# A decoder step on one core: pair 0 of the feed-forward part without Strassen products, and the attention's weight low parts made on VectorE

## The chip, the cores and the metric

The kernel runs on one core of a Trainium2 chip. The time is device microseconds of one execution. Before the change three runs gave 1425.21, 1429.11 and 1429.80 us; the median is 1429.11.

The engines are TensorE (products; PE in the rows, PEld its weight loads), VectorE (DVE), ScalarE (ACT), GpSimd (POOL) and SyncE (SP, whose queue issues nearly all transfers here). Each takes its instructions in the order in which the program gives them.

## The reference, cut to what matters

One layer of a hybrid decoder on 1024 prompt positions and 8 single-position samples, in fp32, model width 1024:

```python
hp = hp + mixer_block(rmsnorm(hp), ...)                      # gMLP heads and SSD heads, one output projection
mk, mv = mem_kv(mem_prompt, norm_mem, w_k, w_v)
hp = hp + cross_attn(rmsnorm(hp), mk, mv, w_q, w_xo)         # 4 heads of 256 into 256 memory tokens
hp = hp + (silu(hn @ w_gate) * (hn @ w_up)) @ w_down         # hn = rmsnorm(hp), hidden width 2816
```

The samples go the same way with caches of keys and values of their own, 256 tokens for each. A last norm follows.

## The kernel before, in words

**Products in two parts.** An fp32 operand is split into a high part, cast to fp32r, and a low part, the difference. A product of two such operands is three products, high by high, high by low, low by high (`mm3`, L164). Weights come in panels of 128 x 1024, eight k-tiles of 128 x 128 side by side. `split_panel` (L139) makes both parts of a panel: ScalarE casts the high part (L146), and the low part (L147) is a subtraction on GpSimd or VectorE. The tags `whi` and `wlo` have three buffers, `raw` two, and `ahead` splits a panel one ahead of its use and loads one more.

**Columns.** Activations stand with features on partitions. The 1032 columns (1024 positions, 8 samples) are chunk 0 (512), chunk 1 (256) and chunk 2 (264).

**Order of the stages.** Memory keys and values, mixer projections with the SSD chunks between, output projection (`wo`), and then the attention in five passes over weight panels: `qc` (queries of chunk 2), `qa` (chunk 0), `qb` (chunk 1), `xoa` (output projection of chunk 0) and `xob` (chunks 1 and 2). While the products of `qa`, `qb` and `xoa` run, the attention of chunk 2, 0 and 1 is threaded between them by `later`, which counts products: scores (`m_sc`), row maximum on VectorE (`mx`), exponential on ScalarE (`ex`), transposes (`m_pt`), split of the probabilities (`pTh` on ScalarE, `pTl` on VectorE), product with the values (`m_pv`), split of its result (`oh`, `ol`). The samples' attention lies in the same passes: in `qa` VectorE multiplies key caches with spread queries (`kc<-kc,qb`, L1000), in `xoa` value caches with spread probabilities (L1102); each needs a transfer of 512 KB for `qb` and two for `kc`. The passes `qa`, `qb` and `xoa` have eight panels each, whose low parts GpSimd makes; those of `qc` and `xob` VectorE makes.

**From attention to FFN.** `norm_evac` (L906) adds each result of `xob` to the residual, sums the squares on VectorE, and after the eighth panel of a chunk asks `lagged_rstd` (L256) for the reciprocal root mean square: the column sums (`m_csn`) are placed `LAG_N[0]` = 14 products later, the transposes that spread the result over the partitions (`m_crn`) `LAG_N[1]` = 20 products behind the sums. Between them lie a square root on ScalarE and five short operations on VectorE, the last of which writes `crvn`. `quarters` then scales the residual into four quarters for each of two column halves q: q = 0 folds columns 0 to 255 and 256 to 511 (chunk 0), q = 1 chunks 1 and 2. A quarter `b11`, `b21`, `b12`, `b22` is a half of the features by a half of those columns. `combine` (L1187) makes the seven operands `P1` to `P7` of a Strassen scheme from them, by four differences and seven splits. The quarters of q = 1 take the buffers of those of q = 0.

**The pairs.** The 22 hidden tiles are 11 pairs. For a pair and a weight (gate `g`, up `u`), `gate_up` (L1255) runs seven products of half the features; `prepare` (L1226) forms the weight's four sums (`ws`, L1237 to L1240) and splits each of the seven weight operands (`fw`, 128 x 512). Sums are made on VectorE for the first four items and on GpSimd for later ones. The evacuations combine the seven results (L1283 to L1298). The items are, in order, `g0` and `u0` for q = 0 alone, then each further pair for both q, and `g0`, `u0` for q = 1 behind pair 6. `xob` ends at about 718 us, item `g0` starts there, and item `u0` at about 739.

**The order of instructions.** The program is written in stages, but a scheduler with a time model puts each engine's instructions in order before the launch; `tc.high_priority()` prefers a group and `later` gives the product behind which a group may be issued. Names with `m_` and `g_` are the two groups of PSUM banks.

The line for the engine of the low parts is L147:

```python
(nc.gpsimd if i == 0 or P_QA <= i < P_XO[1] else nc.vector).tensor_tensor(lo[:, s], r[:, s], f(hi[:, s]), op=ALU.subtract)
```

Of the kernel before, what the change touches and what calls it, by code (L numbers as in the profile page):

```python
# [9 lines left out]
F32R = mybir.dt.float32r  # L10
BF16 = mybir.dt.bfloat16
AF = mybir.ActivationFunctionType
ALU = mybir.AluOpType
# [30 lines left out]
def hymba_step(ctx: ExitStack, tc: tile.TileContext, I, O):  # L44
# [24 lines left out]
    def f(ap):  # L69
        return ap.bitcast(F32)  # L70
# [43 lines left out]
    P_QA = add(I["w_q"], 8)  # L114
    P_QB = add(I["w_q"], 8)
    P_XO = [add(I["w_xo"], 8) for _ in range(2)]
    NPAIR = NF // 2

    raws, split = {}, {}
# [19 lines left out]
    def split_panel(i):  # L139
        if i in split or i >= len(panels):  # L140
            return
        load_panel(i)
        r = raws[i]
        hi, lo = (wp.tile([P, D], F32R, tag=x, name=f"w{x[1]}{i}") for x in ("whi", "wlo"))
        for s in (slice(0, 512), slice(512, D)) if i == 0 else (slice(0, D),):
            nc.scalar.copy(hi[:, s], r[:, s])  # L146
            (nc.gpsimd if i == 0 or P_QA <= i < P_XO[1] else nc.vector).tensor_tensor(lo[:, s], r[:, s], f(hi[:, s]), op=ALU.subtract)  # L147
        n = D // panels[i].shape[1]
        split[i] = (hi.rearrange("p (k n) -> p k n", n=n), lo.rearrange("p (k n) -> p k n", n=n))

# [752 lines left out]

    def norm_evac(accs, H, gi, XN, spill, nm, use=None, tmps=None):  # L906

        acc = {}
        pool = nrm

        def evac(j, ci, ps):
            w = CH[ci][1] - CH[ci][0]
            h = H[ci][j // 4][:, j % 4, :]
            with tc.high_priority():
                nc.vector.tensor_add(h, h, ps)
                if j == 0:
                    acc[ci] = accs[ci].tile([P, 512 if accs[ci] is nrm else w], F32, tag=f"acc{'' if accs[ci] is nrm else ci}", bufs=1, name=f"{nm}acc{ci}")
                    nc.scalar.activation(acc[ci][:, :w], h, AF.Square)
                else:
                    sq = pool.tile([P, 512], F32, tag="nsq", bufs=2, name=f"{nm}sq{ci}_{j}")  # L920
                    nc.scalar.activation(sq[:, :w], h, AF.Square)
                    eng = nc.gpsimd if j < 6 and nm == "n1" else nc.vector
                    eng.tensor_tensor(acc[ci][:, :w], acc[ci][:, :w], sq[:, :w], op=ALU.add)
            if spill is not None and j % 4 == 3:
                nc.sync.dma_start(spill[:, j - 3 : j + 1, CH[ci][0] : CH[ci][1]], H[ci][j // 4])
            if j == 7:
                lagged_rstd(LAG_N, lambda rb: (use or normed)(ci, rb[0]), pool, [[acc[ci]]], ci, 1.0 / D, f"{nm}{ci}")

        def normed(ci, rb):
            w = CH[ci][1] - CH[ci][0]  # L930
            hi = [hs(ci, F32R, f"{nm}h{ci}_{i}") for i in range(2)]
            lo = [hs(ci, F32R, f"{nm}l{ci}_{i}") for i in range(2)]
            for k in range(KT):
                i, kk = k // 4, k % 4
                tmp = n2.tile([P, 512], F32, tag=tmps[0], bufs=2, name=f"{nm}t{ci}_{k}")
                nc.vector.scalar_tensor_tensor(tmp[:, :w], H[ci][i][:, kk, :], vecT[:, k, gi : gi + 1], rb[:, :w], op0=ALU.mult, op1=ALU.mult)
                split_from(hi[i][:, kk, :], lo[i][:, kk, :], tmp[:, :w], nc.gpsimd if k % 2 else None)
            XN[ci] = xof((hi, lo))

        return evac  # L940

    quarters = None
    with ExitStack() as c2:
# [185 lines left out]

        H2 = [None] * 3  # L1130
        n3accs = [nrm] * 3
        ev_xo = norm_evac(n3accs, H2, V_FFN, None, h2_d, "n3", lambda ci, rb: quarters(ci, rb))
        XO = [lambda k, ci=ci: (OS[ci][0][k // 4][:, k % 4, :], OS[ci][1][k // 4][:, k % 4, :]) for ci in range(3)]

        def h2(ci):
# [12 lines left out]
    with ExitStack() as c3:  # L1148
# [8 lines left out]

        def operand(q, nm):

            if nm == ORDER[-1]:  # L1160
                return [n3.tile([P, 4, 264], F32R, tag="op", bufs=4, name=f"s{nm}{x}{q}")[:, :, : WQ[q]] for x in "hl"]
            if q == 0:
# [24 lines left out]
        def combine(q):  # L1187
# [4 lines left out]
                XQ[q][nm] = operand(q, nm)  # L1192
                split_from(*XQ[q][nm], src, eng)

            part("P1", b11)
            nc.vector.tensor_tensor(b11, b12, b11, op=ALU.subtract)
            part("P5", b11)
            nc.vector.tensor_tensor(b11, b22, b11, op=ALU.subtract)
            part("P6", b11)
            part("P2", b21)  # L1200
            nc.vector.tensor_tensor(b12, b22, b12, op=ALU.subtract)
            part("P7", b12)
            nc.vector.tensor_tensor(b21, b21, b11, op=ALU.subtract)
            part("P4", b21)
            part("P3", b22)


        items = [(x, 0, (0,)) for x in "gu"]
        for fp in range(1, NPAIR):
            items += [(x, fp, (0, 1)) for x in "gu"] + ([(x, 0, (1,)) for x in "gu"] if fp == 6 else [])  # L1210
        wraw, wsum, wop = {}, {}, {}
# [9 lines left out]

        def order_of(n):

            return ORDER if n > 3 else ("P1", "P2", "P6", "P7", "P5", "P4", "P3")

        def prepare(step):  # L1226

# [4 lines left out]
            (a11, a12), (a21, a22) = ((t[:, 0:512], t[:, 512:D]) for t in wraw[n])  # L1232
            nm = order_of(n)[o]
            if nm == "P6":
                eng = nc.vector if n < 4 else nc.gpsimd
                s1, s2, s3, s4 = wsum[n] = [n3.tile([P, 512], F32, tag="ws", bufs=4, name=f"ws{n}_{i}") for i in range(4)]
                eng.tensor_tensor(s1, a21, a22, op=ALU.add)  # L1237
                eng.tensor_tensor(s2, s1, a11, op=ALU.subtract)  # L1238
# [76 lines left out]
                    differences.append(lambda q=q, r=res[q]: down_operands(fp, q, r))  # L1315

        differences = []

        def down_operands(fp, q, r):

# [100 lines left out]
            return t[:, 0, i], t[:, 1, i]  # L1421

        stage(plan_of(P_XO[1], 8, first=(1, 2), last=(1, 2), chunks=(1, 2)), XO, ev_xo, name="xob")
        for n in range(len(items)):
            gate_up(n, between_of(n))
        form_differences()
# [212 lines left out]
```

## Time and profile before

| what | value |
|---|---|
| median of three runs | 1429.11 us (1425.21 to 1429.80) |
| profiled execution | 1433.45 us, span 1431.7 us |
| mean granted TensorE clock | 0.984 |
| TensorE busy | 1373.5 us, 96% of the span, 10291 products |
| VectorE busy | 967.6 us, 68% |
| ScalarE busy | 627.3 us, 44% |
| GpSimd busy | 365.5 us, 26% |

The profile is of one execution. The span is from the first to the last instruction; the execution's own time is 1.75 us longer. Busy shares are means over stages with different limits, so the rows below are read stage by stage. The granted clock is a share of 2.4 GHz: 1.00 is 2.4 GHz and 0.50 is 1.2 GHz; a value between is a mean over a stretch. In a row of a group, the number behind the comma is the mean length of one instruction in ns, and behind the second bar stands the idle time of the engine in front of the group. Names are `output<-inputs` with their buffer numbers left out.

### The profile page before, as it was taken

Reading aid. Unit: us, or ns where it says so; the run is one execution under the profiler, and the core shown is the slowest. Engines: PE = TensorE matmul, PEld = TensorE weight load, DVE = VectorE, ACT = ScalarE, POOL = GpSimd, SP = SyncE. Lnnn points to the kernel's source line nnn. Section 1 sums busy time; section 2 is a strip of 40 time slices with the busy share of each in tenths; the row PEclk is TensorE's granted clock in tenths of the full one; section 3 lists DMA queues with packets and bytes.
Section 4 is the critical chain, followed back from the end, with each engine's and each line's share of the span. In section 5 each row is a group of like instructions: output and inputs, shape, how many; then the busy total and the mean of one; then the engine's idle time right before and its main releaser. Section 6 shows DMA issues by size and latency. Waiting matters only on the chain. (4 is left out here: it accounts for less than half of the span.)

```text
span 1431.7 us, 26080 instructions
## 1 busy us (share of the span) xinstructions
PE 1373.5 (96%) x10291; PEld 1308.1 (91%) x10291; DVE 967.6 (68%) x2021; ACT 627.3 (44%) x1141; POOL 365.5 (26%) x289
## 2 busy tenths in 40 slices
PE   8999999999999989999979999999899999999997
PEld 8889988899998968978979999999899999999997
DVE  7875689734524876578988766676765665655685
ACT  5666545234423545744464332232332343544654
POOL 3321122201121524320001434334443431003020
PEclk9999999999999999999999999999999999999998
DMA  8531243311733487377324554434546569655664
GB/s 301 186 96 61 91 126 104 97 45 48 248 133 99 154 288 269 106 269 276 104 89 144 170 159 138 142 118 140 170 159 201 171 189 317 206 184 171 203 194 133
DMA packets 145531, 232.67 MB, mean 163 GB/s; under 512 B 8328, under 2 KB 91880, under 8 KB 145024
## 3 DMA queue, kind: packets, MB, share of 16 engines
q1 hardware_dynamic: 145264, 230.94, 49.8%
q8 instruction: 81, 1.33, 0.4%
q14 instruction: 42, 0.34, 0.1%
q10 hardware_dynamic: 144, 0.05, 0.0%
HBM read 179.16 MB, written 51.81 MB: 161 GB/s over the span
## 5 line engine op out<-in xcount | busy, mean ns | idle before, releaser
L146 ACT CAST wh<-wr 128x1024 fp32r<-128x1024 f32 (+1 forms) x85 | 88.0, 1038 | 85.3 <-PE g_gv L170 25.1
L275 ACT CAST fw<-ws 128x512 fp32r<-128x512 f32 x96 | 59.2, 620 | 137.8 <-POOL ws L1238 61.6
L276 DVE TENSOR_TENSOR fw<-ws,fw 128x512 fp32r<-128x512 f32 x96 | 88.9, 928 | 41.3 <-ACT fw L275 41.0
L147 DVE TENSOR_TENSOR wl<-wr,wh 128x1024 fp32r<-128x1024 f32 x59 | 75.9, 1289 | 28.3 <-ACT wh L146 28.1
L147 POOL TENSOR_TENSOR wl<-wr,wh 128x1024 fp32r<-128x1024 f32 (+1 forms) x26 | 62.8, 2415 | 112.2 <-ACT wh L146 67.3
L275 ACT CAST fw<-fr 128x512 fp32r<-128x512 f32 x72 | 44.5, 618 | 79.5 <-PE m_uZ L170 20.7
L1237 POOL TENSOR_TENSOR ws<-fr 128x512 f32<-128x512 f32 x20 | 26.8, 1341 | 200.4 <-DMA fr<-in_w_gate_dram 120.8
L276 DVE TENSOR_TENSOR fw<-fr,fw 128x512 fp32r<-128x512 f32 x72 | 59.5, 826 | 9.6 <-ACT fw L275 9.1
L1542 PE MATMUL m_d<-xP,dwhi 128*128 128x264 f32 x448 | 64.1, 285 | 0.0
L276 DVE TENSOR_TENSOR dwlo<-dw,dwhi 128x1024 fp32r<-128x1024 f32 x32 | 39.8, 1245 | 35.1 <-ACT dwhi L275 35.0
L1542 PE MATMUL g_d<-xP,dwhi 128*128 128x256 f32 x448 | 63.0, 283 | 0.0
L276 DVE TENSOR_TENSOR xP<-xsP,xP 128x512 fp32r<-128x512 f32 (+2 forms) x84 | 55.0, 696 | 11.4 <-ACT xP L275 9.8
L170 PE MATMUL m_uY<-sP,fw 128*128 128x264 f32 (+1 forms) x432 | 58.4, 284 | 2.1 <-DVE fw L276 1.5
L170 PE MATMUL g_gY<-sP,fw 128*128 128x256 f32 (+1 forms) x432 | 58.4, 283 | 1.7 <-DVE t L1292 1.7
L1542 PEld LDWEIGHTS m_d<-xP,dwhi 128*128 128x128 f32 x448 | 58.5, 189 | 0.0
L1542 PEld LDWEIGHTS g_d<-xP,dwhi 128*128 128x128 f32 x448 | 57.7, 191 | 0.0
L170 PEld LDWEIGHTS m_uY<-sP,fw 128*128 128x128 f32 x432 | 54.6, 189 | 2.7 <-DVE fw L276 1.7
L170 PEld LDWEIGHTS g_gY<-sP,fw 128*128 128x128 f32 x432 | 54.3, 190 | 2.4 <-DVE t L1292 2.3
L1304 POOL TENSOR_TENSOR u<-u,g 128x512 f32<-128x512 f32 (+1 forms) x22 | 30.1, 1372 | 100.4 <-DVE u L1296 99.5
L275 ACT CAST dwhi<-dw 128x1024 fp32r<-128x1024 f32 x32 | 33.6, 1051 | 48.7 <-PE m_d L1542 38.5
L275 ACT CAST xP<-xsP 128x512 fp32r<-128x512 f32 (+2 forms) x84 | 45.2, 588 | 21.4 <-DMA xsP<-x_d 12.2
L170 PE MATMUL m_gY<-sP,fw 128*128 128x264 f32 x360 | 49.2, 285 | 4.9 <-DVE t L1292 4.9
(520 smaller groups left out, 3918.5 us busy)
## 6 DMA issues: line engine op xcount, KB each, us to landing
xsP<-x_d SPq DMA_DIRECT2D x35, 520.0 KB, 5.6
wr<-in_w_q_dram SPq DMA_DIRECT2D x24, 512.0 KB, 4.0
fr<-in_w_gate_dram SPq DMA_DIRECT2D x24, 512.0 KB, 3.6
fr<-in_w_up_dram SPq DMA_DIRECT2D x24, 512.0 KB, 3.7
dr<-in_w_down_dram SPq DMA_DIRECT2D x22, 512.0 KB, 6.4
s_d<-ds SPq DMA_DIRECT2D x22, 512.0 KB, 3.2
wr<-in_w_in_dram SPq DMA_DIRECT2D x20, 512.0 KB, 4.0
dw<-s_d SPq DMA_DIRECT2D x20, 512.0 KB, 4.5
```

The source lines that it names most:

```text
L146: nc.scalar.copy(hi[:, s], r[:, s])
L147: (nc.gpsimd if i == 0 or P_QA <= i < P_XO[1] else nc.vector).tensor_tensor(lo[:, s], r[:, s], f(hi[:, s]), op=ALU.subtract)
L170: ins = nc.tensor.matmul(ps, lhs(k)[a], rhs(k)[b], start=(fresh and i == 0), stop=(i == n - 1), skip_group_check=not (fresh and done))
L275: nc.scalar.copy(dst_hi, src)
L276: (eng or nc.vector).tensor_tensor(dst_lo, src, f(dst_hi), op=ALU.subtract)
L1237: eng.tensor_tensor(s1, a21, a22, op=ALU.add)
L1304: nc.gpsimd.tensor_tensor(t, t, gates[q][:, 1, :, :], op=ALU.mult)
L1542: nc.tensor.matmul(ps[:, : WQ[q]], wdn[n](k)[a], x_at(nm, q, k)[b], start=(i == 0), stop=(i == 3 * NPAIR - 1))
```

## The change

Two things change. Pair 0 on q = 0 leaves the Strassen scheme: its four panels (two of `w_gate`, two of `w_up`) are split as other panels are, and `first_pair`, which stands between `xob` and the remaining items, multiplies each with both column halves, whose operands are the split quarters `P1`, `P2` (half 0) and `B12`, `P3` (half 1). `combine(0)` makes these four splits first and the differences behind them; `B12` is new and lies in two of the four `gu` buffers. The sums for items `g1` and `u1` stay on VectorE. The spread of the third norm is placed 44 products behind its sums in place of 20. And the low parts of all panels but the first are made on VectorE.

```diff
+    P_G0 = add(I["w_gate"], 2)
+    P_U0 = add(I["w_up"], 2)
...
-            (nc.gpsimd if i == 0 or P_QA <= i < P_XO[1] else nc.vector).tensor_tensor(lo[:, s], r[:, s], f(hi[:, s]), op=ALU.subtract)
+            (nc.gpsimd if i == 0 else nc.vector).tensor_tensor(lo[:, s], r[:, s], f(hi[:, s]), op=ALU.subtract)
...
-                lagged_rstd(LAG_N, lambda rb: (use or normed)(ci, rb[0]), pool, [[acc[ci]]], ci, 1.0 / D, f"{nm}{ci}")
+                lagged_rstd(lag, lambda rb: (use or normed)(ci, rb[0]), pool, [[acc[ci]]], ci, 1.0 / D, f"{nm}{ci}")
...
-        ev_xo = norm_evac(n3accs, H2, V_FFN, None, h2_d, "n3", lambda ci, rb: quarters(ci, rb))
+        ev_xo = norm_evac(n3accs, H2, V_FFN, None, h2_d, "n3", lambda ci, rb: quarters(ci, rb), lag=(14, 44))
...
+            if nm == "B12":
+                return [n3.tile([P, 4, 264], F32R, tag="gu", bufs=4, name=f"s{nm}{x}{q}")[:, :, : WQ[q]] for x in "hl"]
...
-            part("P1", b11)
+            if q == 0:
+
+                for nm, b in (("P1", b11), ("P2", b21), ("B12", b12), ("P3", b22)):
+                    part(nm, b)
+            else:
+                part("P1", b11)
...
-        items = [(x, 0, (0,)) for x in "gu"]
+        items = []
...
-            return ORDER if n > 3 else ("P1", "P2", "P6", "P7", "P5", "P4", "P3")
+            return ORDER if n > 1 else ("P1", "P2", "P6", "P7", "P5", "P4", "P3")
...
-                eng = nc.vector if n < 4 else nc.gpsimd
+                eng = nc.vector if n < 2 else nc.gpsimd
...
+        def first_pair():
+
+            for x, p0 in (("g", P_G0), ("u", P_U0)):
+                r = piece(f"{x}0_0")[:, :, :256].rearrange("p (j h) n -> p j h n", j=2)
+                for j in range(2):
+                    ahead(p0 + j)
+                    if p0 + j == P_U0:
+                        load_pair(0)
+                    if p0 + j == P_U0 + 1:
+                        for s in range(3):
+                            prepare(s)
+                    hi, lo = split[p0 + j]
+                    for half in range(2):
+                        ps = (gbank, mbank)[half](f"{x}0_{j}_{half}")
+                        ops = [XQ[0][nm] for nm in (("P1", "P2"), ("B12", "P3"))[half]]
+                        mm3(ps[:, :256], lambda k: (hi[:, k, :], lo[:, k, :]), lambda k: tuple(t[:, k % 4, :] for t in ops[k // 4]), range(KT))
+                        with tc.high_priority():
+                            if x == "g":
+                                nc.scalar.activation(r[:, j, half, :], ps[:, :256], AF.Silu)
+                            else:
+                                nc.vector.tensor_mul(r[:, j, half, :], gates[0][:, j, half, :], ps[:, :256])
+                gates[0] = r if x == "g" else None
+            differences.append(lambda: down_operands(0, 0, r))
...
         stage(plan_of(P_XO[1], 8, first=(1, 2), last=(1, 2), chunks=(1, 2)), XO, ev_xo, name="xob")
+        first_pair()
```

## Rows read from the trace of the kernel before

**Rows 1.** Stretches: length; busy PE, PEld, DVE, ACT, POOL (instructions); clock; transfer share; GB/s.

```profile
500.00:560.00 60.00, 52.90 (x276) 44.21 (x275) 43.66 (x162) 27.66 (x59) 18.07 (x9) 0.97 0.89 306
...
560.00:606.00 46.00, 46.00 (x379) 45.36 (x378) 22.93 (x59) 34.96 (x91) 21.47 (x9) 1.00 0.35 107
...
606.00:660.00 54.00, 50.58 (x268) 42.66 (x267) 42.52 (x149) 23.92 (x60) 12.30 (x5) 0.94 0.86 301
...
660.00:718.00 58.00, 58.00 (x451) 56.28 (x450) 52.55 (x117) 25.87 (x41) 0.25 (x2) 1.00 0.43 135
...
725.00:740.00 15.00, 5.67 (x45) 5.42 (x44) 12.26 (x34) 9.38 (x13) 0.00 (x0) 0.83 0.22 70
...
515.00:520.00 5.00, 4.69 (x18) 3.95 (x19) 1.70 (x5) 2.55 (x6) 1.78 (x1) 0.66 0.90 340
...
630.00:635.00 5.00, 5.00 (x12) 3.94 (x13) 4.94 (x23) 2.80 (x8) 0.00 (x0) 0.50 0.85 261
```

**Rows 2.** Waits of TensorE, 720 to 790: total us, times, longest.

```profile
PE m_crn L279 <- DVE crvn L224: 8.0, 1, 8.0
PE g_gY L170 <- DVE t L1292: 1.3, 1, 1.3
PE g_gX L170 <- DVE fw L276: 1.1, 1, 1.1
```

**Rows 3.** Instructions in order of time, 717 to 745: start us, length us.

```profile
723.81 0.50 PE L236 MATMUL m_csn<-ones,n3acc 128*128 128x1 f32 x4
...
729.27 0.16 DVE L224 RECIPROCAL crvn<-rsan 128x2 f32<-128x2 f32 x1
...
730.32 0.73 PE L236 MATMUL m_csn<-ones,n3acc 128*128 128x1 f32 x6
...
738.76 0.18 DVE L224 RECIPROCAL crvn<-rsan 128x3 f32<-128x3 f32 x1
...
739.61 2.67 PE L170 MATMUL m_uX<-sP,fw 128*128 128x256 f32 x12
```

**Rows 4.** Chain of waits: start us, us, what (a group of twelve products).

```profile
1140.70 1.43 PE g_uX L170 x12
```

**Rows 5.** VectorE groups, 718 to 748 and (last) 660 to 718: busy us, mean ns.

```profile
L276 DVE TENSOR_TENSOR fw<-ws,fw 128x512 fp32r<-128x512 f32 x7 | 4.8, 689 | 0.0
...
L1237 DVE TENSOR_TENSOR ws<-fr 128x512 f32<-128x512 f32 x2 | 1.4, 681 | 0.1
...
L1285 DVE TENSOR_TENSOR t<-t,g_gY 128x256 f32<-128x256 f32 x1 | 0.4, 423 | 0.0
...
L147 DVE TENSOR_TENSOR wl<-wr,wh 128x1024 fp32r<-128x1024 f32 x8 | 9.8, 1223 | 0.0
```

**Rows 6.** Waits of TensorE, 500 to 560 and (last) 610 to 660.

```profile
PE m_pv L170 <- DVE pTl L276: 3.5, 3, 2.0
...
PE m_pt L279 <- DVE pTl L276: 0.9, 1, 0.9
...
PE g_xoa L170 <- ACT ex L1028: 2.9, 1, 2.9
```

**Rows 7.** Instructions in order of time, 524 to 536: GpSimd beside VectorE.

```profile
526.70 2.59 POOL L147 TENSOR_TENSOR wl<-wr,wh 128x1024 fp32r<-128x1024 f32 x1 [6.09 <-ACT wh L146]
...
526.96 2.62 DVE L1000 SCALAR_TENSOR_TENSOR kc<-kc,qb 128x256 f32<-128x256 f32 x1
```

**Rows 8.** VectorE groups: 500 to 560 (first), 606 to 660 (two), 660 to 718 (two).

```profile
L1000 DVE SCALAR_TENSOR_TENSOR kc<-kc,qb 128x256 f32<-128x256 f32 x64 | 31.9, 561 | 8.2 <-DMA qb<-q_d 8.2
...
L1102 DVE SCALAR_TENSOR_TENSOR kc<-kc,qb 128x256 f32<-128x256 f32 x50 | 23.4, 524 | 6.1 <-DMA qb<-p_d 6.1
...
L923 DVE TENSOR_TENSOR n3acc<-n3acc,n3sq 128x512 f32<-128x512 f32 x4 | 5.6, 1405 | 0.7 <-ACT n3sq L921 0.7
...
L1102 DVE SCALAR_TENSOR_TENSOR kc<-kc,qb 128x256 f32<-128x256 f32 x14 | 5.1, 424 | 0.0
...
L923 DVE TENSOR_TENSOR n3acc<-n3acc,n3sq 128x512 f32<-128x512 f32 x3 | 2.1, 698 | 0.0
```

More of the change, by code (lines that the diff above doesn't have):

```diff
@@ L901, in hymba_step, with norm_evac @@
         stage([([(P_GU + j, j)], (0, 1, 2)) for j in range(2)] + [([(P_GU + j, j) for j in (2, 3)], (0, 1, 2))], X, ev_um, name="gu")
-    def norm_evac(accs, H, gi, XN, spill, nm, use=None, tmps=None):
+    def norm_evac(accs, H, gi, XN, spill, nm, use=None, tmps=None, lag=LAG_N):
         acc = {}
@@ L1199, in combine @@
             part("P6", b11)
-            part("P2", b21)
+            if q == 1:
+                part("P2", b21)
             nc.vector.tensor_tensor(b12, b22, b12, op=ALU.subtract)
@@ L1204, in combine @@
             part("P4", b21)
-            part("P3", b22)
-        items = [(x, 0, (0,)) for x in "gu"]
+            if q == 1:
+                part("P3", b22)
+        items = []
         for fp in range(1, NPAIR):
```

## The prediction

> **What bounds the kernel now.** I first read the stretches of the attention and of the passage into the feed-forward part (FFN) [rows 1]: in the pass `qb` (560 to 606) and in the last projection pass `xob` (660 to 718) TensorE is busy all the time; in `qa` (500 to 560) it misses 7.1 us, in `xoa` (606 to 660) 3.4 us, and from 725 to 740 it works for 5.67 us of 15. So products bound this kernel, and what can be won are the holes. The reader is to see in these rows that VectorE is the engine beside the holes: 52.55 of 58 us in `xob`, 12.26 of 15 in the largest hole. The waits of TensorE after 720 come next [rows 2]: 8.0 us for `crvn`, the reciprocal root mean square of the last column chunk, and 1.3 and 1.1 us for sums and weights that VectorE was late with. The order of time inside that hole [rows 3] shows why: the column sums of the chunk are done at 731.05, `crvn` at 738.94, because ScalarE and VectorE had the first pair's Strassen work in front of it, while TensorE had the transposes of `crvn` next in its order and nothing it could take instead. The waits of the attention passes [rows 6] and the durations of VectorE's sample products there [rows 7, 8] are the second field.
>
> **Part 1: the first pair by plain products.** TensorE: before, gate and up of pair 0 on columns 0 to 255 and 256 to 511 folded together are 2 x 7 groups of 12 products, 168; after, 2 weights x 2 panels x 2 halves x 24, 192. A group of 12 takes 1.43 us [rows 4], so 24 more cost **+2.9 us**, all on the path.
>
> VectorE: it loses 14 low parts of 0.69 (9.7), eight sums of 0.68 (5.4) and 11 evacuations of 0.42 (4.6); it gains four panel low parts of 1.22 (4.9), one operand split more, `B12` (1.2), and four gate products of 0.42 (1.7) [rows 5]. That is 19.7 less against 7.8 more, 11.9 us of relief between about 700 and 750, where it is full. Besides, the combined operands of columns 0 to 511 (four differences and their four splits) are not due at 718 any more but when pair 1 begins, some 25 us later. That relief is cover, and no term of its own: it lets the waits of 1.3 and 1.1 us go and keeps the operands of columns 512 to 1031 from becoming late, though pair 1 starts earlier. ScalarE's work shrinks as well (four wide casts for 14 narrow ones, one operand more), GpSimd loses two products, and SP issues four weight loads of 512 KB as before, panels in place of pairs, so I cost these at nothing; the cover is that all three have idle time here, and without it a late weight would cost what rows 2 show for one, 1.1 us. `B12` sits in two of the four buffers of gate results, which the results of pair 1 take next; these are first written two groups after pair 0's last product, so nothing waits.
>
> The wait for `crvn`: 192 products that need nothing from that chunk now lie behind the sums, and the transposes are placed 44 products behind them in place of 20. That is 5.3 us at 0.119 each, where before it was 2.4. The two chains from sums to `crvn` in the trace took 5.1 (724.31 to 729.43) and 7.9 us (731.05 to 738.94) [rows 3]. At 5.3 us the first fits and the second would leave 2.6. So of 8.0 + 1.3 + 1.1 us of waits, and 1.1 us that the first group behind the hole lost at the low clock (2.67 us against 1.43 plus its tail [rows 3, 4]; granted 0.83 on average from 725 to 740 [rows 1], so part of it at 1.2 GHz), 11.5 in all, 2.6 stay. **Part 1: 2.9 - 11.5 + 2.6 = -6.0 us.** Ends: -8.6 with no wait left, +0.5 with the 8.0 and the 1.1 back.
>
> **Part 2: low parts on VectorE.** 24 panels (`w_q` twice, `w_xo` once) move, each 1.22 us there [rows 5], so VectorE gets 29.3 us. What it loses shows in rows 7: the GpSimd operation runs from 526.70 to 529.29, and the sample product that VectorE started inside it took 2.62 us, where a like product takes 0.42 with GpSimd idle [rows 8]. By the means [rows 8], 64 products in `qa` lost (561 - 424) ns each, 8.8 us; 50 in `xoa` 5.0; four square sums there (1405 - 698) ns, 2.8. So 16.6 us of stretching go, and the net is +12.7 us of VectorE time.
>
> Where it lies: in `qb` VectorE is busy for 22.93 of 46 us and TensorE waits for nothing [rows 1], so eight low parts there cost nothing; if that idle time were gone they would cost up to 9.8. In `qa` 8.8 us go and 9.8 come, but a stretch always falls on a product with a softmax step queued behind it, while the low part can stand in the 16 us in which VectorE is idle there (it is made long before use: three buffers deep, and no wait of TensorE names it). In `xoa` GpSimd makes five low parts [rows 1], so 6.1 us come and 7.8 go. No row shows the new order of VectorE's queue, so I bound the gain: at best all waits that have a stretched chain in front go, 3.5 + 0.9 in `qa` and 2.9 in `xoa` [rows 6], and with them the low clock behind (0.66 and 0.50 of 5 us [rows 1], 1.7 and 2.5 us): 11.5. At worst 0, and below that the third rival. I take about half, 3.0 for `qa` and 2.5 for `xoa` (1.7 us of net relief and some of the clock), nearest to the row of stretched products that the waits follow. **Part 2: -5.5 us.**
>
> The plain exchange of engine time speaks against this part: 29.3 us more on an engine that is nearly full in `xoa`, for 16.6. The Trainium skill's page "Perfetto Trace Analysis", section "Optimizing Scalar/DVE Operations", says that work may well go from a saturated VectorE to GpSimd, though the two share an SBUF read port, so that moving between them might not help. By its first half the part would cost up to the third rival's price, by its second nothing. This trace agrees with the second half: 2.62 against 0.42 us.
>
> **Sum.** -6.0 - 5.5 = -11.5 us. The profiled execution took 1433.45 us (span 1431.7), so 1421.9 for a like one; that execution is 4.3 above the median of 1429.11, and against the median the forecast is **1417.6 us**. A measurement of this kernel tells some 0.3%, 4.3 us, from no change.
>
> **Rivals.**
> *The low parts win nothing.* For it: the chains in `qa` also wait for the sample loads, with the transfer engines busy for 0.89 of that stretch [rows 1]; what VectorE gains it would then wait for data. Against: TensorE's waits stand behind stretched products, not behind the loads alone. Only part 1 counts: 1429.1 - 6.0 = 1423.1.
> *The norm's wait stays.* If ScalarE's table changes between SiLU and square root or the eight products of chunk 1 get into the chain again, it takes longer than 44 products cover, and the 8.0 + 1.1 return: part 1 is +0.5, with part 2 1424.1, without it 1429.6. For it: 7.9 us is longer than 5.3. Against: VectorE has 11.9 us less to do.
> *VectorE's queue becomes the bound (slower).* In `qa` and `xoa` each low part is 1.22 us in front of a row maximum or a low part of probabilities, and TensorE waits for it. It decides where the chain has no slack left, as the waits of 3.5, 0.9 and 2.9 show for some places; with all 13 exposed, 15.9 - 6.0 = +9.9, 1439.0. Against: GpSimd's operation held the same queue for longer. That first half of the page's sentence points here; I give it no more than the rows do.
>
> **Chances.** Forecast 0.50; nothing from part 2 0.22; norm's wait 0.14; queue 0.12; something unseen 0.02. The range runs from near the best ends (1429.1 - 8.6 - 11.5 = 1409) to the norm's wait without part 2 (1429.6): 1411 to 1430, which leaves out the queue and a little below. Faster by over 0.3% (under 1424.8): 0.50 + 0.18 of the second case + 0.05 of the third = 0.73. Within 0.3%: 0.04 + 0.09 + 0.02 = 0.15. Slower: 0.12.
>
> **What would show it.** Right: TensorE busy without a hole of over 3 us between 715 and 750, pair 0 as 192 products, the wait for `crvn` at 2.6 us or less; sample products at a mean near 424 ns in `qa` and `xoa`, the wait of 2.9 us in `xoa` under 2 and no stretch at half clock behind it. Wrong: a wait of 5 us or more for `crvn`, TensorE waiting for `pTl` or `ex` more than 7.3 us in `qa` and `xoa` together, or any wait for `wl`. The forecast fails outright if the FFN's later pairs, which I take as unchanged, get new waits for weights.

## The result, and the profile after

The changed kernel takes **1412.06 us** (median of 4 runs, 1410.90 to 1412.72), the kernel before, run beside it, 1429.45 us (4 runs, 1425.21 to 1432.05). The ratio is **0.9872**, 95% interval 0.9854 to 0.989: 18.3 us of 1429 are gone (15.7 to 20.9), where the prediction said 11.5. The profiled execution took 1412.27 us (span 1410.4). Two more measurements of the same program, in the experiments below, gave 0.9854 and 0.9861.

The page of the changed kernel, part 1: busy time of each engine, its share, instructions.

```profile
PE 1369.1 (97%) x10315; PEld 1305.8 (93%) x10315; DVE 957.9 (68%) x2021; ACT 626.1 (44%) x1131; POOL 304.1 (22%) x263
```

The kernel before had 10291 products on TensorE; 24 more are there, 192 in place of 168 for the first pair. GpSimd lost 61 us of work. VectorE, which spends 29 us on what it took over, is not busier (957.9 against 967.6 us): the plain pair takes 11.6 us off it (956.0 in e1 below), and the rest is made up by operations that are no longer stretched.

The stretches of the changed kernel: first and last us, length, busy time of the engines, granted clock, DMA share. They are cut where TensorE starts its first product of `qa`, `qb`, `xoa`, `xob`, of the first pair and of the second.

```profile
489.60:551.10 61.50, 58.43 (x308) 48.85 (x306) 49.37 (x181) 31.97 (x67) 3.63 (x3) 1.00 0.88 315
551.10:587.90 36.80, 36.80 (x314) 36.78 (x313) 24.36 (x46) 26.42 (x64) 0.00 (x0) 1.00 0.49 159
587.90:658.20 70.30, 68.92 (x400) 59.83 (x399) 57.58 (x208) 36.08 (x90) 0.00 (x0) 1.00 0.73 263
658.20:708.00 49.80, 49.38 (x410) 48.99 (x409) 43.70 (x82) 26.13 (x40) 0.25 (x2) 1.00 0.43 138
708.00:732.50 24.50, 24.50 (x209) 24.50 (x208) 18.21 (x42) 15.77 (x22) 0.00 (x0) 1.00 0.29 88
```

The same cuts in the kernel before:

```profile
489.40:557.00 67.60, 60.50 (x307) 50.24 (x306) 51.51 (x174) 32.08 (x67) 25.68 (x13) 0.97 0.85 295
557.00:596.90 39.90, 39.90 (x340) 39.87 (x339) 18.13 (x43) 29.57 (x72) 19.46 (x8) 1.00 0.42 136
596.90:670.80 73.90, 70.47 (x387) 60.20 (x386) 59.86 (x207) 34.91 (x87) 14.71 (x6) 0.95 0.71 250
670.80:718.10 47.30, 47.30 (x398) 47.30 (x397) 41.85 (x77) 21.91 (x34) 0.25 (x2) 1.00 0.44 131
```

Work slides from one pass into its neighbour (`qb` lost 3.1 us and `xob` gained 2.5 while TensorE was busy nearly all through), so only the sum of the four passes compares well: 228.7 us before, 218.4 after, **10.3 us less**. In the traces of the two further measurements of this program (e3, e11) the passes take 216.1 and 215.9 us, 12.6 and 12.8 less. The first pair takes 24.5 us without a gap; before, from its first product to the second pair's first it was 30.0, with two groups of twelve (2.9) still to come, so 32.9: **8.4 us less**. Both stretches of low clock, 0.97 in `qa` and 0.95 in `xoa`, are gone. The rest of the FFN differs by 3 us between the two profiled executions: TensorE's listed waits behind 740 us sum to 17.1 us before and 14.2 after, spread over many small ones.

Waits of TensorE in the changed kernel, 489 to 740: total, times, longest. These are all of them.

```profile
PE m_pt L281 <- ACT ex L1041: 2.4, 2, 1.6
PE m_pv L172 <- DVE pTl L278: 1.0, 1, 1.0
PE m_pv L172 <- ACT pTh L277: 0.5, 1, 0.5
PE g_xob L172 <- ACT oh L277: 0.4, 1, 0.4
PE m_pv L172 <- ACT ex L1030: 0.4, 1, 0.4
```

Of the 3.5 us for `pTl` [rows 6] 1.0 are left; the 2.9 for `ex` in front of `xoa` [rows 6] and the 8.0 for `crvn` [rows 2] have no successor. Why there is none for `crvn` shows in TensorE's and VectorE's order of time (start, length):

```profile
712.16 0.50 PE L238 MATMUL m_csn<-ones,n3acc 128*128 128x1 f32 x4
...
716.31 0.38 PE L281 MATMUL m_crn<-ident,crvn 128*128 128x128 f32 x2
716.53 0.73 PE L238 MATMUL m_csn<-ones,n3acc 128*128 128x1 f32 x6
...
722.90 0.18 DVE L226 RECIPROCAL crvn<-rsan 128x3 f32<-128x3 f32 x1
...
723.63 0.49 PE L281 MATMUL m_crn<-ident,crvn 128*128 128x128 f32 x3
```

From the last column sum (717.26) to `crvn` (723.08) it is still 5.8 us, against 7.9 [rows 3], but TensorE has the plain pair's products for all of it.

VectorE's groups after, `qa` (first two) and `xoa` (last two): busy us, mean ns, idle before.

```profile
L1002 DVE SCALAR_TENSOR_TENSOR kc<-kc,qb 128x256 f32<-128x256 f32 x64 | 23.2, 419 | 8.0 <-DMA qb<-q_d 7.8 <-DVE pTl L278 0.3
L149 DVE TENSOR_TENSOR wl<-wr,wh 128x1024 fp32r<-128x1024 f32 x9 | 11.0, 1217 | 2.0 <-ACT wh L148 2.0
...
L1104 DVE SCALAR_TENSOR_TENSOR kc<-kc,qb 128x256 f32<-128x256 f32 x64 | 23.2, 418 | 7.6 <-DMA qb<-p_d 7.6
...
L925 DVE TENSOR_TENSOR n3acc<-n3acc,n3sq 128x512 f32<-128x512 f32 x6 | 4.1, 679 | 0.0
```

The sample products went from 561 and 524 ns to 419 and 418, the square sums from 1405 to 679 [rows 8].

### The profile page after: what moved, and what is told of

Read it like the earlier page. It is cut to its first block, busy times and chain, and to the rows that moved or that the text cites. A ratio compares the mean times of both kernels' runs of the same rounds, so it can differ in the third digit from the quotient of the medians.

```text
span 1410.4 us, 26083 instructions
## 1 busy us (share of the span) xinstructions
PE 1369.1 (97%) x10315; PEld 1305.8 (93%) x10315; DVE 957.9 (68%) x2021; ACT 626.1 (44%) x1131; POOL 304.1 (22%) x263
## 5 line engine op out<-in xcount | busy, mean ns | idle before, releaser
L149 DVE TENSOR_TENSOR wl<-wr,wh 128x1024 fp32r<-128x1024 f32 x87 | 109.1, 1256 | 34.6 <-ACT wh L148 34.3
L148 ACT CAST wh<-wr 128x1024 fp32r<-128x1024 f32 (+1 forms) x89 | 92.2, 1038 | 85.3 <-PE g_gv L172 25.1
L277 ACT CAST fw<-ws 128x512 fp32r<-128x512 f32 x88 | 54.4, 622 | 125.9 <-POOL ws L1249 54.8
L278 DVE TENSOR_TENSOR fw<-ws,fw 128x512 fp32r<-128x512 f32 x88 | 81.1, 923 | 38.3 <-ACT fw L277 38.2
L277 ACT CAST fw<-fr 128x512 fp32r<-128x512 f32 x66 | 40.8, 619 | 80.3 <-PE m_uZ L172 20.1
L278 DVE TENSOR_TENSOR xP<-xsP,xP 128x512 fp32r<-128x512 f32 (+2 forms) x84 | 54.9, 694 | 12.8 <-ACT xP L277 12.3
L278 DVE TENSOR_TENSOR dwlo<-dw,dwhi 128x1024 fp32r<-128x1024 f32 x32 | 39.8, 1245 | 34.7 <-ACT dwhi L277 34.6
L172 PE MATMUL m_uY<-sP,fw 128*128 128x264 f32 x396 | 53.7, 284 | 1.4 <-DVE fw L278 1.4
L172 PE MATMUL g_gY<-sP,fw 128*128 128x256 f32 (+1 forms) x396 | 53.1, 283 | 0.0
L172 PEld LDWEIGHTS m_uY<-sP,fw 128*128 128x128 f32 x396 | 50.1, 189 | 1.7 <-DVE fw L278 1.7
L172 PEld LDWEIGHTS m_gY<-sP,fw 128*128 128x128 f32 x360 | 45.6, 188 | 5.0 <-DVE t L1303 4.7
L172 PEld LDWEIGHTS g_gY<-sP,fw 128*128 128x128 f32 x396 | 49.7, 190 | 0.3
L172 PE MATMUL g_uY<-sP,fw 128*128 128x256 f32 x360 | 48.3, 283 | 1.7 <-DVE t L1303 1.0
```

What stands on the lines that cost most here:

```text
L149: (nc.gpsimd if i == 0 else nc.vector).tensor_tensor(lo[:, s], r[:, s], f(hi[:, s]), op=ALU.subtract)
L172: ins = nc.tensor.matmul(ps, lhs(k)[a], rhs(k)[b], start=(fresh and i == 0), stop=(i == n - 1), skip_group_check=not (fresh and done))
L277: nc.scalar.copy(dst_hi, src)
L278: (eng or nc.vector).tensor_tensor(dst_lo, src, f(dst_hi), op=ALU.subtract)
```

## The experiments

All ratios are to the kernel before, run on the same chip beside the experiment.

**e1: the first pair alone.** The changed kernel, in which GpSimd makes the low parts of `QA`, `QB` and the first `XO` again:

```diff
-            (nc.gpsimd if i == 0 else nc.vector).tensor_tensor(lo[:, s], ...)
+            (nc.gpsimd if i == 0 or P_QA <= i < P_XO[1] else nc.vector).tensor_tensor(lo[:, s], ...)
```

> The plain first pair and the later spread alone; the 24 low parts go back to GpSimd. Theory (each part pays by itself, the attention passes gained through VectorE's freed queue): the passage from xob to pair 1 keeps its 8.3 us, the passes qa to xob fall back to about 229 us from 218, so 8 to 11 us under the kernel before, ratio 0.992 to 0.995. Rival (the first pair's relief of VectorE is what shortened the passes too): ratio about 0.987, as the full change.

Measured: 1423.21 us, **0.9953** (0.9936 to 0.9969), so 6.7 us less than before (4.4 to 9.1). That is a little less than the 8 to 11 us expected. The waits in the passes are back and the first pair has none (the longest waits of TensorE, 486 to 745, and the stretch of the first pair):

```profile
PE m_pv L172 <- DVE pTl L278: 3.4, 4, 1.2
PE g_xoa L172 <- ACT ex L1030: 2.9, 1, 2.9
PE m_pt L281 <- ACT ex L1041: 2.3, 1, 2.3
PE m_pt L281 <- DVE pTl L278: 2.0, 1, 2.0
...
716.60:741.10 24.50, 24.50 (x209) 24.50 (x208) 17.50 (x41) 13.10 (x20) 0.00 (x0) 1.00 0.27 87
```

The four passes take 228.8 us from `qa`'s first product to the first pair, 228.7 before. The pair takes 24.5 us, TensorE busy throughout at clock 1.00. So the change's first part is worth what it does to the pair and the norm, and nothing of it reaches back.

**e2: the low parts alone.** The kernel before with only the line above as the change has it.

> The low parts on VectorE alone; the first pair stays Strassen, the spread 20 products behind. Theory: the passes qa to xob take about 218 us as after the change, the wait of 8 us for crvn stays, 8 to 11 us under the kernel before, ratio 0.992 to 0.995, with sample products at 415 to 430 ns. Rival (VectorE's extra 29.8 us are felt when the first pair does not relieve it): ratio 0.998 to 1.003.

Measured: 1416.67 us, **0.9906** (0.9885 to 0.9926), 13.4 us less (10.6 to 16.4), more than the 8 to 11 expected. Its waits from 486 to 745 begin with

```profile
PE m_crn L279 <- DVE crvn L224: 6.6, 1, 6.6
PE g_gX L170 <- DVE fw L276: 1.2, 1, 1.2
PE m_pt L279 <- ACT ex L1039: 0.6, 1, 0.6
```

and the stretches of `qa` and `xoa` read

```profile
489.00:548.90 59.90, 58.23 (x309) 49.00 (x307) 49.11 (x181) 32.05 (x67) 3.57 (x3) 1.00 0.89 319
...
585.60:655.10 69.50, 68.92 (x400) 59.88 (x399) 58.77 (x214) 37.16 (x92) 0.00 (x0) 1.00 0.73 266
```

The passes take 215.0 us, 13.7 less, and that is where all of the gain lies. It can be counted: time without a product fell in `qa` from 7.1 to 1.7 us and in `xoa` from 3.4 to 0.6, 8.3 us; and the same 1432 products of the four passes keep TensorE busy for 212.8 us in place of 218.2, 5.4 us, where the clock had been 0.97 and 0.95 (a part of either stretch at 1.2 GHz) and is 1.00 now. The two parts together, 6.7 + 13.4 = 20.1 us, are near the 18.3 to 20.9 of the three measurements of the whole change, so they add.

**e3: the distance of the spread.**

```diff
-        ev_xo = norm_evac(..., lag=(14, 44))
+        ev_xo = norm_evac(..., lag=(14, 20))
```

> The changed kernel with the third norm's spread 20 products behind its sums, not 44. Theory (the chain from sums to crvn takes 6 us or more and the place in TensorE's order decides): a wait of 3 to 4 us for crvn comes back, ratio to the kernel before 0.990 instead of 0.987. Rival (with plain products to take, the scheduler sets the spread by its own clock anyway): no wait over 1 us, ratio as the full change.

Measured: 1407.36 us, 0.9854 (0.9825 to 0.9883). Compared instruction by instruction, the two programs have the same order on all five engines, apart from buffer numbers: the number in the call moves nothing here. In both the transposes lie 31 and 54 products behind the sums of the two chunks, neither 20 nor 44; that the scheduler sets them by its own estimate of when `crvn` is there is likely, but no run shows it. So this run says nothing of the distance; it is a second measurement of the changed kernel, and shows that 0.2% lies between two measurements of one program.

**e4: `qb` back on GpSimd.**

```diff
-            (nc.gpsimd if i == 0 else nc.vector)...
+            (nc.gpsimd if i == 0 or P_QB <= i < P_XO[0] else nc.vector)...
```

> The changed kernel with the eight low parts of qb alone back on GpSimd. Theory of the prediction (in qb VectorE idles half the time and TensorE waits for nothing, so it does not matter where these are made): within 1 us of the full change. Rival (GpSimd's hold on VectorE's operations delays the softmax chain there too, and qa and qb each lost about 3 to 6 us by it): 2 to 4 us over the full change.

Measured: 1407.52 us, 0.9847 (0.9826 to 0.9869), passes 214.9 us. With the eight low parts of `qb` on either engine the time is the same within the measurement, and TensorE is busy all through `qb` in both (39.80 of 39.8 us here). What counts of the change's second part lies in `qa` and `xoa`.

**e5: GpSimd works as before, for nothing.** The changed kernel, and besides it GpSimd repeats each of the 24 subtractions into a tile that nobody reads:

```diff
+            if P_QA <= i < P_XO[1]:
+                nc.gpsimd.tensor_tensor(junk[0].tile(...), r, f(hi), op=ALU.subtract)
```

> The changed kernel, in which GpSimd makes each of the 24 low parts a second time, into a tile that nobody reads; VectorE makes the ones that are used. No engine waits for GpSimd's copies except the buffers of the raw weights, which are three deep. Theory (GpSimd's operation on two SBUF operands stops VectorE's operations on two SBUF operands for its length): the sample products of the pass qa come back to a mean near 560 ns, TensorE's waits of about 3 us in qa and xoa return with the half clock behind them, and VectorE carries its 29 us besides; ratio 0.995 to 1.01, at least 13 us above the changed kernel's 1412. Rival A (what was won is the length of GpSimd's operation in the weight chain, 2.4 us against 1.22): nothing in the chain waits for GpSimd any more, so 1408 to 1414, 0.985 to 0.989. Rival B (the gain came from another order of the program): the same 1408 to 1414.

Measured: 1436.30 us, **1.0038** (1.0026 to 1.0049), some 25 us above the changed kernel, whose three ratios average 0.9862. Nobody reads what GpSimd makes; still the passes take 241.4 us. One GpSimd operation and VectorE beside it, in order of time (start, length):

```profile
539.63 0.41 DVE L1006 SCALAR_TENSOR_TENSOR kc<-kc,qb 128x256 f32<-128x256 f32 x1
...
539.64 2.67 POOL L152 TENSOR_TENSOR junk<-wr,wh 128x1024 bf16<-128x1024 f32 x1 [8.31 <-ACT wh L149]
...
539.98 3.40 DVE L150 TENSOR_TENSOR wl<-wr,wh 128x1024 fp32r<-128x1024 f32 x1
```

VectorE's groups in its `qa` (489.5 to 561), busy us, mean ns, idle before:

```profile
L1006 DVE SCALAR_TENSOR_TENSOR kc<-kc,qb 128x256 f32<-128x256 f32 x64 | 31.4, 543 | 1.5 <-DMA qb<-q_d 1.5
L150 DVE TENSOR_TENSOR wl<-wr,wh 128x1024 fp32r<-128x1024 f32 x9 | 14.9, 1659 | 2.0 <-ACT wh L149 2.0
...
L281 DVE TENSOR_TENSOR pTl<-m_pt,pTh 128x256 fp32r<-128x256 f32 x8 | 3.3, 412 | 0.8 <-ACT pTh L280 0.8
L1032 DVE TENSOR_REDUCE mx<-m_sc 128x1 f32<-128x256 f32 x8 | 3.3, 408 | 0.0
```

A subtraction that takes 1.21 us alone began at 539.98 and ended at 543.38, 1.07 us after GpSimd's at 542.31: VectorE stood still until GpSimd was nearly or quite done. It is so with the others too: the ten sample products that were held in e5 and the eight in the kernel before all ended 0.28 to 0.29 us behind GpSimd's operation, and the seven low parts held in e5 1.08 us behind it, though between 1.1 and 2.4 us of GpSimd's operation were still to come when they began. Held are the operations that read two tiles of SBUF (`kc`, `wl`, and the split of the queries, 2.30 us in place of 1.25). Those that read PSUM, `pTl` and the row maximum, have their usual 412 and 408 ns. TensorE's waits follow: 10.5 us for `pTl` in the passes, the longest 6.5. It waits also 1.6 us for a weight's cast. A second reader keeps the raw weight longer in its buffer (there are two of these, not three as the expectation has it), so late weights are a rival for the 25 us; but ScalarE waits for raw weights of the passes no longer than in the changed kernel, 11.7 against 13.3 us in all (480 to 735), so this rival does not hold.

**e6: GpSimd only writes.** In e5's place, a fill of the tile with zeros.

> The control to e5_gp_repeats: at the same 24 places GpSimd only fills the unused tile with zeros, so it reads no SBUF operand. Theory: VectorE is not held, the sample products stay near 420 ns, ratio 0.984 to 0.989. Rival C (any work of GpSimd at these places costs, by its issue, its semaphores or its writes): sample products above 480 ns in qa and a ratio above 0.991.

Measured: 1409.90 us, 0.9864 (0.9842 to 0.9886), passes 215.6 us, sample products 420 and 422 ns. But nothing held the fills back, and all 24 (0.95 us each) were done between 481 and 509 us; for the later panels this is no control. So it was made again as e9.

**e7: the low part twice on VectorE.** The second one goes into the unused tile; GpSimd has none of it.

```diff
+            if P_QA <= i < P_XO[1]:
+                nc.vector.tensor_tensor(junk[0].tile(...), r, f(hi), op=ALU.subtract)
```

> The changed kernel, in which VectorE makes each of the 24 low parts twice, the second time into a tile that nobody reads: 29.3 us more of VectorE time in the same queue, without GpSimd. It prices VectorE's time in these passes. Theory (29.3 us were taken on at no cost because the queue had room once it was not held; by the rows of the changed kernel VectorE is busy for 49 of 61 us in qa, 24 of 37 in qb and 58 of 70 in xoa, so 10 more fit into qa, 10 into qb and 6 into xoa): 0 to 6 us more than the changed kernel, ratio 0.986 to 0.992, less than what e5_gp_repeats costs. Rival D (each low part stands in front of a softmax step with its whole length): 16 of them in qa and xoa at 1.22 us, up to 16 us, ratio near 0.999.

Measured: 1422.74 us, **0.9946** (0.9929 to 0.9962), 12 us above the changed kernel. This lies between the two expectations, above the 0.992 of the theory's and below the rival's 0.999: 27.5 us more of VectorE's time (985.4 against 957.9 over the run) came with 12 us. They are not a clean price of VectorE's time. Waits of TensorE from 486 to 720, and ScalarE's for raw weights from 480 to 735:

```profile
PE m_pv L175 <- ACT pTh L280: 3.3, 2, 2.8
PE m_pv L175 <- DVE pTl L281: 2.6, 2, 2.0
PE g_xob L175 <- ACT wh L149: 1.8, 2, 1.5
...
ACT wh L149 <- DMA wr<-in_w_xo_dram: 15.6, 6, 5.5
ACT wh L149 <- DMA wr<-in_w_q_dram: 14.3, 10, 3.1
```

and the stretches of `qb` and `xob`:

```profile
543.40:583.60 40.20, 36.83 (x294) 36.29 (x293) 35.81 (x72) 26.48 (x58) 0.00 (x0) 0.94 0.63 216
...
657.00:715.20 58.20, 54.21 (x426) 53.16 (x427) 49.77 (x104) 30.58 (x50) 0.25 (x2) 0.94 0.40 132
```

ScalarE waits for raw weights for 29.9 us, where it is 13.3 in the changed kernel: the second subtraction frees the raw weight's buffer later (the loads wait 92.3 us for VectorE's two subtractions, 50.2 for the one of the changed kernel). Softmax steps slid into `qb` and `xob`, TensorE waited 1.5 to 2.8 us at a time, and the granted clock fell to 0.94 in both, with a part at 1.2 GHz. How much of the 12 us is VectorE's time and how much the late weights is not separated.

**e9: GpSimd only writes, at the panels' places.** ScalarE writes one column of the unused tile behind each panel's cast, then GpSimd fills the tile three times:

```diff
+            if P_QA <= i < P_XO[1]:
+                jt = junk[0].tile(...)
+                nc.scalar.copy(jt[:, :1], hi[:, :1])
+                for _ in range(3):
+                    nc.gpsimd.memset(jt, 0.0)
```

> A better control to e5_gp_repeats than e6_gp_writes_only, whose fills were all done between 481 and 509 us because nothing held them back. Here each of the 24 fills is tied to its weight panel (ScalarE writes one column of the unused tile behind the panel's cast, then GpSimd fills the tile three times, near 2.8 us, as long as its subtraction took in e5_gp_repeats). GpSimd is as busy beside VectorE as there, but reads nothing. Theory (two SBUF operands against two SBUF operands): sample products near 420 ns in qa and xoa, no wait of TensorE over 2 us in the passes, ratio 0.983 to 0.989. Rival C (GpSimd's activity as such holds VectorE): sample products at 480 ns or more, ratio 0.995 to 1.005, as in e5_gp_repeats.

Measured: 1411.98 us, **0.9868** (0.9832 to 0.9904), passes 216.5 us. GpSimd's and VectorE's instructions: duration least, median and greatest in ns, first and last start.

```profile
L155 POOL MEMSET junk<- x72: 944/951/960, 488.0 to 644.1; 128x1024 bf16 x72
...
L1009 DVE SCALAR_TENSOR_TENSOR kc<-kc,qb x64: 415/422/426, 509.9 to 547.2; 128x256 f32<-128x256 f32 x64
...
L1111 DVE SCALAR_TENSOR_TENSOR kc<-kc,qb x64: 404/422/426, 612.8 to 657.9; 128x256 f32<-128x256 f32 x64
```

GpSimd was busy for 68 us in all beside the same passes, and not one of 128 sample products took over 426 ns. Its activity as such costs nothing.

**e10: GpSimd reads one operand.**

```diff
+            if P_QA <= i < P_XO[1]:
+                jt = junk[0].tile(...)
+                nc.gpsimd.tensor_copy(jt, f(hi))
```

> As e5_gp_repeats, but GpSimd copies the high part of each panel into the unused tile: one SBUF operand in place of two. Theory as it stands says nothing of one operand. If GpSimd's reading of SBUF as such holds VectorE: sample products at 480 ns or more on the mean with single ones over 1 us, ratio above 0.993. If two operands on GpSimd's side are needed: sample products near 420 ns and a ratio of 0.983 to 0.989. I expect the first, at 0.6.

Measured: 1411.18 us, **0.9865** (0.9837 to 0.9893). I gave 0.6 to the outcome with a loss; in the time there is none. In the trace the hold is there, only shorter. GpSimd's copy and the samples of `qa`, duration least, median and greatest in ns:

```profile
L153 POOL CAST junk<-wh x24: 1040/1233/2127, 483.8 to 637.2; 128x1024 bf16<-128x1024 f32 x24
...
L1007 DVE SCALAR_TENSOR_TENSOR kc<-kc,qb x64: 400/420/1302, 503.7 to 543.9; 128x256 f32<-128x256 f32 x64
```

One copy and the sample product behind it, in order of time:

```profile
513.51 1.13 POOL L153 CAST junk<-wh 128x1024 bf16<-128x1024 f32 x1 [6.10 <-ACT wh L149]
...
514.00 0.92 DVE L1007 SCALAR_TENSOR_TENSOR kc<-kc,qb 128x256 f32<-128x256 f32 x1
```

The sample product that began inside the copy (513.51 to 514.64) took 0.92 us, ending 0.28 after it. Over `qa` the samples' mean is 458 ns and over `xoa` 473, some 40 and 55 ns above the changed kernel's: 6 us of stretching in all, where e5 had 7.9 in `qa` and 10.4 in `xoa` on the samples alone. The reading of one operand holds VectorE too, but the copy is over in 1.23 us (the median) where e5's subtraction took 2.82, and holds of that length were hidden here.

**e8 and e12: a candidate, and e11: the changed kernel again.** The candidate leaves `qb`'s low parts on GpSimd (as e4) and takes the odd low parts of the first norm's operands, which GpSimd makes from 455 to 490 us, to VectorE as well:

```diff
-                split_from(hi[i][:, kk, :], lo[i][:, kk, :], tmp[:, :w], nc.gpsimd if k % 2 else None)
+                split_from(hi[i][:, kk, :], lo[i][:, kk, :], tmp[:, :w], None)
```

> A version that might beat the changed kernel: qb's eight low parts stay on GpSimd, as in e4_qb_on_gpsimd, and the nine low parts of the first norm's operands that GpSimd makes between 455 and 490 us go to VectorE. Theory (the lock acts there too: TensorE has a wait of 2.0 us at 455 to 470 and a granted clock of 0.89 there in the changed kernel): 0 to 3 us below e4_qb_on_gpsimd, 1405 to 1409, ratio 0.983 to 0.986. Rival (VectorE is busy for 13.2 of 15 us there and becomes late itself): 1 to 6 us above it, ratio 0.986 to 0.990.

> The changed kernel once more, beside the same runs of the kernel before, to set e4_qb_on_gpsimd and e8_candidate against it: if those two gain what their rows say (6 us less VectorE time in the passes), its ratio is 0.9855 to 0.988, above e8_candidate's 0.9828; if the differences of 0.3 per cent are only those between runs, as e3_spread_at_20 suggests, it is 0.983 to 0.9855.

> The kernel of e8_candidate once more. If it is faster than the changed kernel, whose three measurements stand at 0.9872, 0.9854 and 0.9861, its ratio is 0.984 or less, with its interval below 0.9861; if e8_candidate's 0.9828 was the spread between runs, 0.985 to 0.987.

Measured: the candidate 1405.70 us, 0.9828 (0.9806 to 0.9849), and again 1404.22 us, **0.9808** (0.9785 to 0.9832); the changed kernel again 1409.08 us, 0.9861 (0.9827 to 0.9895). That is what the last expectation asked for: both intervals of the candidate lie below all three ratios of the changed kernel (0.9854 to 0.9872), though they overlap the intervals of two of these, and the two kernels never ran beside each other. So it is faster, by some 0.4%, as far as ratios of separate measurements tell. Where the second edit acts, TensorE's wait for the norm's operand fell from 2.0 us to 0.8, and the granted clock from 455 to 470 us is 1.00 in place of 0.89 (in the trace of e8). How much of the gain is this and how much `qb`'s low parts is not separated; these alone (e4) stand at 0.9847.

## Why the prediction was right, and by how much it missed

The sign and both mechanisms held, and the time lies in the range (1411 to 1430), but only just: 1412.06 is 1.1 us above its lower end, and the two further measurements of the same program (1407.36 and 1409.08) lie below it. That the range held is luck. The time came out 5.5 us below the forecast, nearly all of it in part 2, and no rival stood on that side.

**Part 1, -6.0 us: held.** e1 measures -6.7 (4.4 to 9.1). The terms +2.9 for 24 products and -11.5 for the waits and the clock behind them make -8.6, and in the traces the pair's stretch shrank by 8.4; e1's time alone can't tell this from -6.0. The term that failed is the +2.6 us "left" of the wait: no wait is left. It rested on "the transposes are placed 44 products behind them in place of 20", and e3 shows that this number moves nothing. It did not give the order before either: between the sums that end at 731.05 and their transposes [rows 3, rows 2] TensorE had no product at all, not 20, and in the changed kernel it has 54. In the changed kernel the distance from the last sum to the transposes is 6.4 us, just behind the chain's 5.8. The rival with the norm's wait asked whether 44 products cover 7.9 us; that was the wrong question. e2, without the plain pair, keeps 6.6 of the 8.0 us, so the plain pair is what removed it, and the low parts are not; the chain still takes 5.8 us, and the pair's products cover it.

**Part 2, -5.5 us: right mechanism, the size less than half.** e2 measures -13.4 (10.6 to 16.4). The step that failed is "I take about half": of the ends 0 and -11.5 the far one was nearer. What the term left out, in the order of size:
- Nearly all of the waits that had a stretched chain in front went, as the best end had it (1.0 us of 7.3 is left in e2), and in e2 a further one went down with them, which the prediction left out. It is this one of the kernel before, from 489 to 730:

```profile
PE m_pt L279 <- ACT ex L1039: 2.6, 2, 2.2
```

It is 0.6 us in e2 and 0.5 in e4, but 0.3, 1.7 and 2.4 in three traces of one program, the changed kernel (e3, e11 and the first), so a good part of it is chance. Whether the hold was behind it stays open: ScalarE's idle time in front of that line, put down to VectorE's reciprocal `sm`, did not fall (8.3 us before, 12.5 in e2, 15.7 in the changed kernel).
- The clock. I read 4.2 us of it from two slices of 5 us; over the whole passes the same products were busy for 5.4 us longer, all of which came back in e2. A wait of 3 us cost its own length and some more behind it.
- VectorE's net time. I worked out 16.6 us of stretching from two groups (samples and square sums) and so a net of +12.7 us. Over the run VectorE is at 971.3 us in e2 against 967.6 before, +3.7: by that some 25.6 us of stretching went (the three traces of the changed kernel differ among themselves, 957.9 to 963.5). The other groups that read two SBUF tiles were held as well; the splits of the first norm's operands, for one, I had not counted.

**The place of `qb`'s low parts at no cost: held**, by e4, within 0.3%.

**The rivals.** "The low parts win nothing" fell with e2; VectorE waits for the sample loads in `qa` and `xoa` as before (7.8 and 7.6 us, where it was 8.2 and 6.1), but TensorE doesn't stand behind that. "VectorE's queue becomes the bound" fell as forecast, though perhaps with less to spare than I thought: doing the same work on it once more costs 12 us in e7, late weights included. The Trainium skill's page "Perfetto Trace Analysis", section "Optimizing Scalar/DVE Operations", says that offloading some work from a saturated VectorE, even to GpSimd, may make sense, but might not help between these two. The first half of that rule would have had the change the other way; here the work went from GpSimd to a VectorE that was busy for 81% of `xoa`, and 13.4 us were won.

**Why moving work onto the busier engine wins** is the question of e5, e7, e9 and e10. Against the changed kernel, the same 24 subtractions done once more cost 25 us on GpSimd (e5) and 12 us on VectorE, late weights included (e7); fills of the same length on GpSimd cost nothing (e9) and reads of one operand nothing that can be measured (e10). So it is not GpSimd's activity, nor the length of its operation in the weights' chain, since in e5 nobody reads what it makes: it is that VectorE is held while GpSimd reads. It is not VectorE's total time either. The kernel before lost some 25.6 us to holds, and e2, which spends 29.2 us on the low parts instead, is 13.4 us faster. (In e5, where VectorE's own low parts can be held as well, VectorE is busy for 38.2 us more than in the changed kernel.) What differs shows in ScalarE's waits for the row maximum `mx`, on which the exponential depends, from 480 to 735 us before, after, in e5 and in e7:

```profile
ACT ex L1028 <- DVE mx L1026: 35.1, 12, 6.6
...
ACT ex L1030 <- DVE mx L1028: 14.7, 10, 3.6
...
ACT ex L1034 <- DVE mx L1032: 35.8, 16, 6.4
...
ACT ex L1034 <- DVE mx L1032: 16.3, 8, 4.4
```

With holds the softmax chain waits some 35 us for VectorE, without them 15, and a second set of low parts on VectorE adds hardly anything. Why the two kinds of lost time fall so differently is an argument that no run shows: a hold starts when a weight is cast, wherever VectorE is, while a low part has a place in VectorE's order that was chosen with the softmax steps in view. The Trainium skill's page "SBUF — State Buffer", section "Who interferes with whom", has the rule: a VectorE instruction with two SBUF inputs contends with a GpSimd instruction that reads SBUF, not with one that only writes it, and whichever starts second is stopped for the whole of the other. The runs agree where VectorE is second: 3.40 in place of 1.21 us in e5, at most 426 ns in e9, up to 1302 ns in e10.

**What would show it right or wrong.** No hole over 3 us between 715 and 750, no wait for `crvn`, samples at 419 and 418 ns against the 424 forecast, the wait of 2.9 us in `xoa` gone and the clock at 1.00: all came. The waits for weights (`fw`) behind 740 us sum to 4.5 us against 4.9 before; one of 1.0 us, in front of a `g_uX`, is new, so this sign held in the sum only.

## What to carry to other kernels

Before work is given to GpSimd because VectorE is full, look for VectorE operations on two SBUF tiles beside it whose longest duration is that of GpSimd's operation (here 2.62 against 0.42 us): a VectorE operation that starts inside one of GpSimd's waits for its end, and VectorE doing the work itself can be the cheaper, even where it takes more of VectorE's time in all (here 29.2 us for some 25.6 of holds). What may stay on GpSimd is, by these runs, work that only writes (e9), that is short (e10), or that lies beside no chain that TensorE waits for (e4); VectorE operations on PSUM beside it were not held (e5). And count a wait of TensorE with the clock that falls behind it, over the whole stage and not in the slice of the wait alone.

## What the runs showed of the hardware that was not expected

- GpSimd's copy of one operand (1.04 us at the least) holds VectorE as its subtraction of two does (2.39 at the least), to its own end; I had expected a loss from it in the time, and 24 holds of that length showed none (0.9865 against 0.9862).
- Held VectorE operations lose more than once: in e5 the low parts that VectorE made itself were held as well, 1659 ns on the mean in `qa` against 1217.
- Held VectorE operations end at a fixed distance behind GpSimd's operation, whatever was left of it: 0.28 to 0.29 us for 18 sample products (normally 0.42 long), 1.08 for seven low parts (normally 1.21), in e5 and the kernel before.
- Most waits of TensorE of 2 to 3 us go with a lower granted clock in the stretch, a part of it at 1.2 GHz (0.95 in `xoa` before, 0.94 in `qb` and `xob` in e7), but not all: in the kernel before, the 2.23 us that ended at 504.83 are followed by 1.00 from 505 to 510, the 1.98 that ended at 515.22 by 0.66 from 515 to 520. In the changed kernel, whose longest wait there is 1.6 us, it is 1.00 in all four passes. In the kernel before the products' lower clock made 5.4 of the 13.7 us that e2 won in the passes.
